# Hybrid encoder layer: four changes at the seams between stages, and three PSUM banks for scores with two for wide products

## Chip, cores and metric

One core of one Trainium2 chip runs the whole kernel. The metric is the device time of one execution in microseconds; of several executions the median is taken.

## What is computed

One layer of a bidirectional hybrid encoder on 1024 tokens of width 1024, all in float32:

```
h    = RMSNorm_pre(x);  z = h @ W_in   (q | f_fwd | f_bwd | i | g | u | v | gate_a | gate_b)
A    = bidirectional gated linear recurrence, 8 heads, 128x128 state per head (scores inside chunks, state between them)
Bm   = u * (128-position mixing matrix per channel group applied to LayerNorm(gelu(v)))
mix  = (sigmoid(gate_a) * (A @ W_a) + sigmoid(gate_b) * (Bm @ W_b)) @ W_out
x    = x + RMSNorm_post(mix)
x    = x + RMSNorm_post(SwiGLU(RMSNorm_pre(x)))            hidden width 2816
x    = x + (p @ W_ple) * sigmoid(x @ W_ple_gate)
```

## The kernel before

Every wide product keeps float32 accuracy with three matmuls: each operand is split into a high and a low part (`split_into`, L113 to L115: ScalarE copies the high part, VectorE subtracts for the low one), and `mm3` (L127) adds high-high, high-low and low-high. One 128x512 output with 1024 contracted elements is 24 matmuls.

PSUM has eight banks. `PS_BUFS` (L51) gives three to the tag mm, two to sc, one each to tr, st and o. `ps_any` (L58) hands wide products the tags mm, sc, mm, st, mm, sc in rotation; `wide_at` counts its uses, so whoever uses it shifts the tags of everything after.

The tile framework takes priorities from the order of the program, orders each engine's instructions with a simulation of its own, and gives buffers out as they come free in it. The order of an engine in the trace is therefore not that of the source, and on the chip each engine keeps to the order it was given. A pool on the left or right side of SBUF lies on the pools opened before it on that side; a tile of a new pool waits for the tiles that lay in the same place.

The stages, in order:

- **Opening.** `load_pw` (L318) loads and splits halves of p (transposed) and w_ple, 512 KB each, and `ple_product` (L392) makes 16 tiles of p @ W_ple from them, through the banks mm, st, mm, o. They are copied into four slots of `h32[1][1]` and stored to `pr_d`. `norm_x` (L345) normalises and transposes x through the sc banks.
- **Token-major products.** `tm_group` (L383) makes v (gelu, LayerNorm into vn), i, u and the second half of i. `u` and `vn` (L418) take the places of the split p and w_ple, u first. L439 to L445 mix positions and multiply into u.
- **First seam.** After the last `tm_group` (L447), L451 to L458 transpose u's eight tiles and split them into `bT`; `branch_b` (L468) loads a block of W_b, splits it and multiplies it with both halves of bT. The operands T1 to T4 of the next stage (L485 to L496) are made on VectorE in between. The memory of `raw` and `whl` (L460, L461) is where u and vn lay.
- **Columns and FFN gates.** `Seven.product` (L247) makes four 128x512 tiles from seven products of half the contraction (Strassen-Winograd), 12 matmuls each. X accumulates products 1, 6, 7, 4 in an mm bank, Y 5 and 3 in an sc bank, Z product 2 in `zbank` (st, tr, o in turn, L233). Product 1 and 2 need only original operands, product 5 needs T1, product 6 T2, product 7 T3 and product 4 T4. `begin` (L237) does products 1 and 2 ahead for the first two column pairs of the FFN.
- **Heads.** For each of 8 heads `scores` (L589) runs seven levels; a level is four matmuls of 128x128 per half (L612) into an sc bank, then VectorE updates QA (L621) and X (L624) in place or into a new buffer, merges the bank into SC (L634, for the two last levels ScalarE at L631), ScalarE copies the middle (L645) and GpSimd makes Y (L648). `proj` (L549) makes the next head's gates in four tiles through mm banks; ScalarE empties them at L579 and L580 into F, of which there is one buffer, and sk, of which there are two. `outputs` (L658) follows. In the last head `gate_a` (L726) fills in.
- **Merge.** `merge` (L762) multiplies with W_a (`whl` and `raw` have two buffers each) and loads W_out (`load_wo`, L777), whose split parts lie where the heads' buffers were. `mix_half` (L784), with `to_fm1` (L814) for the second half, normalises, adds x and transposes through the banks tr and o.
- **FFN and end.** L862 to L878 begin the first two column pairs and make T2, T3 and T4; then gates, down products, and the last gate.

Of the kernel before, what the change touches and what calls it, by code (L numbers as in the profile page):

```python
# [9 lines left out]
F32 = mybir.dt.float32  # L10
F32R = mybir.dt.float32r
# [6 lines left out]
P = 128  # L18
# [17 lines left out]
def kernel(ctx: ExitStack, tc: tile.TileContext, a: dict, out: bass.AP):  # L36
# [11 lines left out]
    dram = ctx.enter_context(tc.tile_pool(name="dram", bufs=1, space=DRAM))  # L48
    psum = ctx.enter_context(tc.tile_pool(name="psum", bufs=1, space=PSUM))

    PS_BUFS = {"mm": 3, "sc": 2, "tr": 1, "st": 1, "o": 1}  # L51
    wide = ["mm", "sc", "mm", "st", "mm", "sc"]
    wide_at = [0]

# [3 lines left out]
    def ps_any():  # L58
        tag = wide[wide_at[0] % len(wide)]
        wide_at[0] += 1  # L60
        return ps_tile(tag)

    def phase(name, bufs=1, side=None):
        pool = tc.tile_pool(name=name, bufs=bufs, reuse_waits="tile", **({"side": side} if side else {}))
        return pool, pool.__enter__()

    def close(*pools):
        for pool in pools:
            pool.__exit__(None, None, None)
# [3 lines left out]
    def t2(pool, role, bufs=2):  # L73
        return pool.tile([P, NH], F32, name=role, tag=role, bufs=bufs)
# [38 lines left out]
    def split_into(hi, lo, src, eng=None):  # L113
        nc.scalar.activation(hi, src, AF.Copy)  # L114
        (eng or nc.vector).tensor_tensor(out=lo, in0=src, in1=hi.bitcast(F32), op=ALU.subtract)  # L115
# [58 lines left out]
    class Seven:  # L174
# [59 lines left out]
            self.n += 1  # L234
            return ps_tile(self.zbanks[self.n % len(self.zbanks)])

        def begin(self, lhs, HB):  # L237

            X = ps_tile("mm")
            self.add(lhs, HB, 1, X, True)  # L240
            c11 = self.keep("p1", X)
            Z = self.zbank()
            self.add(lhs, HB, 2, Z, True)
            nc.vector.tensor_tensor(out=c11, in0=Z, in1=c11, op=ALU.add)
            return X, c11
# [41 lines left out]
    def pair(pool, name, tag):  # L287
# [4 lines left out]
    c_h32, p_h32 = phase("h32", side="right")  # L292
    h32 = [[p_h32.tile([P, 4, NH], F32, name=f"h32_{n}{g}") if n == 0 or g == 1 else None for g in range(2)]
           for n in range(2)]
    c_sgu, sgu = phase("sgu")
    masks = p01.tile([P, len(LEVELS), P], U8, name="masks")
    c_x, p0x = phase("p0x", 3)
    c_r, p0r = phase("p0r", 3)
    c_w, p0w = phase("p0w", 6)
    c_t, p0t = phase("p0t", 2)  # L300
# [17 lines left out]
    def load_pw(i, n):  # L318
        raw = praw[i][:, n]
        nc.sync.dma_start(raw, a[("pT", "w_ple")[i]][n])  # L320
        split_into(pwt[i][:, n, 0], pwt[i][:, n, 1], raw)

    load_pw(0, 0)
    load_x(0)
    load_pw(1, 0)
    nc.sync.dma_start(ident, a["ident"])
    gmix = p0x.tile([P, D], F32, name="gmix", bufs=1)
    nc.sync.dma_start(gmix, a["norm_mix_pre"].partition_broadcast(P))
# [40 lines left out]
    def ev_i(half):  # L369
        def f(t, ps):  # L370
            s = t2(p0t, "vs", 2)
            nc.scalar.activation(s, ps, AF.Copy)
            nc.sync.dma_start(v_d[half * 4:half * 4 + 4, :, t, :].rearrange("h p v -> p h v"),
                              s.rearrange("p (h v) -> p h v", h=4))
        return f
# [4 lines left out]
    def load_tm(gi, kk):  # L380
        return load_split(a["w_tm"][gi, kk], [2, NH], nc.gpsimd if kk % 2 else nc.vector, p0w, p0r)

    def tm_group(w, per_tile, ahead=None):  # L383

        for t in range(NT):
            ps = ps_tile(("mm", "st", "mm", "o", "mm")[t % 5]) if ahead is x_ahead else ps_any()
            mm3(ps, fm_lhs(hT[t // 4], t % 4), lambda p, k: w[k // 2][:, p, k % 2, :], KD)
            if ahead is not None:
                ahead(t)
            per_tile(t, ps)  # L390
# [24 lines left out]
    for t in range(4, NT):  # L415
        for e in range(2):
            ple_product(e, t)
    u, vn = [sgu.tile([P, NT, SGW], F32, name=name, tag="uv", bufs=2) for name in ("u", "vn")]  # L418

    def x_ahead(t):  # L420
        if t + 3 < NT:
# [11 lines left out]
    mf = p0x.tile([P, len(LEVELS), P], F32, name="mf", tag="xt")  # L433
    nc.sync.dma_start(mf, a["masks"])
    nc.vector.tensor_copy(masks, mf)
    tm_group(w, ev_i(0), layer_norm)
    w = [load_tm(2, kk) for kk in range(4)]
    tm_group(w, ev_u)
    for g in range(SGG):  # L439
        ps = ps_any()  # L440
        es = slice(g * SGE, (g + 1) * SGE)
        pv = ps.rearrange("p (c e) -> p c e", e=SGE)
        nc.tensor.matmul(pv, lhsT=wst[:, g, :], rhs=vn[:, :, es], start=True, stop=True)
        nc.vector.scalar_tensor_tensor(out=u[:, :, es], in0=pv, scalar=sgb[:, g:g + 1], in1=u[:, :, es],
                                       op0=ALU.add, op1=ALU.mult)  # L445
    w = [load_tm(3, kk) for kk in range(4)]
    tm_group(w, ev_i(1))  # L447
    close(c_t, c_w, c_r, c_x)


    c_b, p1b = phase("p1b", side="right")  # L451
    bT = [p1b.tile([P, 4, T], F32R, name=f"bT{p}") for p in range(2)]
    for t in range(NT):
        tp = ps_any()
        for i in range(4):
            nc.tensor.transpose(tp[:, i * P:(i + 1) * P], u[:, t, i * P:(i + 1) * P], ident)
        split_into(bT[0][:, :, t * P:(t + 1) * P], bT[1][:, :, t * P:(t + 1) * P],
                   tp.rearrange("p (k t) -> p k t", k=4))  # L458
    close(c_sgu)
    c_raw, rawp = phase("raw", 2)  # L460
    c_whl, whlp = phase("whl", 2)  # L461
# [3 lines left out]
    st1 = Seven(None, rawp, p1t, None, ("st", "tr", "o"))  # L465
    st1.first = whlp

    def branch_b(j):  # L468
        raw = rawp.tile([P, KD, P], F32, name="raw", tag="raw")
        nc.sync.dma_start(raw[:, 0:4], a["w_b"][j])  # L470
        wb = whlp.tile([P, 2, KD, P], F32R, name="whl", tag="whl")[:, :, 0:4]
        split_into(wb[:, 0], wb[:, 1], raw[:, 0:4])
        for n in range(2):
            ps = ps_any()
            mm3(ps, lambda p, k: wb[:, p, k, :], lambda p, k: bT[p][:, k, n * NH:(n + 1) * NH], 4)
            s = t2(p1t, "o", 2)
            nc.scalar.activation(s, ps, AF.Copy)
            nc.sync.dma_start(bw_d[j, :, n * NH:(n + 1) * NH], s)

    branch_b(0)  # L480
    branch_b(1)

    b11, b21, b22 = h32[0][0], h32[0][1], h32[1][1]
    b12 = [hT[1][p][0].bitcast(F32) for p in range(2)]
# [10 lines left out]
        nc.vector.tensor_tensor(out=sb[:, 1], in0=b21[:, k], in1=sa[:, 1], op=ALU.subtract)  # L495
        split_into(T4[0][:, k], T4[1][:, k], sb[:, 1])  # L496
    for j in range(2, KD):
        branch_b(j)
    close(c_b, c_h32)


    c_r, p1r = phase("p1r", 2)
# [234 lines left out]
    for h in range(H):  # L737
        nxt = Head()
        scores(h, cur)
        if h + 1 < H:  # L740
            proj(nxt, h + 1, "qfbg")
        if h == H - 1:

            gate_a(0)
            A0 = new_fm("A0")
            load_A(0, A0, range(H - 1), 5)
            gate_a(1)
            A1 = new_fm("A1")
        outputs(h, cur)
        cur = nxt  # L750
    load_A(1, A1, range(H - 1), 5)
# [9 lines left out]

    def merge(A):  # L762
        for j in range(KD):
            w = load_split(a["w_a"][j], [KD, P], None, whlp, rawp)
            for n in range(2):
                ns = slice(n * NH, (n + 1) * NH)
                ps = ps_any()
                mm3(ps, lambda p, k: w[:, p, k, :], fm_rhs(A[n]), KD)
                sg = t2(t3, "sg", 2)
                nc.sync.dma_start(sg, sig_d[j, :, ns])  # L770
                m0 = t2(t3, "y", 4)
                nc.sync.dma_start(m0, m0_d[j, :, ns])
                nc.vector.tensor_tensor(out=sg, in0=ps, in1=sg, op=ALU.mult)
                nc.vector.tensor_tensor(out=M[:, j, ns], in0=sg, in1=m0, op=ALU.add)
            load_wo(j)
# [84 lines left out]
    st4.w, st4.second, st4.t, st4.ev = s4w, s4r, t4, evp  # L860

    lhs = ahead[0]()  # L862
    begun = [st4.begin(lhs, HB2)]
    lhs1 = ahead[1]()
    begun.append(st4.begin(lhs1, HB2))

    b12, b22 = h1f
    for k in range(4):
# [199 lines left out]
```

## Time and profile before

| | |
|---|---|
| Median of 3 runs | 1988.57 us (1987.51 to 1992.4) |
| The profiled execution | 1992.11 us, of which the span of its instructions is 1990.3 us |
| TensorE, matmuls | 1926.7 us busy, 97% |
| TensorE, weight loads | 1604.8 us, 81%, beside the matmuls |
| VectorE, ScalarE, GpSimd | 56%, 38%, 10% |
| Mean granted TensorE clock | 0.989 |
| DMA | 201.87 MB, mean 101 GB/s |

The profile divides the span into 40 slices. TensorE is in its top tenth in nearly all of them; the slices that are lower are the first one, the stretch of the heads, and the seams. The granted clock is given in tenths of full speed, 2.4 GHz; 0.5 is 1.2 GHz.

### The profile page before, as it was taken

The numbers are of one execution on the slowest core, as the hardware profiler recorded it, in microseconds if no ns is written. First come the engines' busy times: TensorE is split into PE (matmuls) and PEld (weight loads), VectorE is DVE, ScalarE is ACT, GpSimd is POOL, SyncE is SP. The second block draws the span as 40 slices with busy tenths as digits, with TensorE's granted clock in tenths as the row PEclk, the third lists the DMA queues.
The fourth block names the chain that finished last, engine by engine and source line by source line (L and its number), as shares of the span: only waits on it lengthen the run. The fifth ranks groups of instructions, "written<-read, shape, count | busy, mean of one in ns | idle before, by whom it ended". The sixth has DMA issues, their size and how long they took to land.

```text
span 1990.3 us, 24039 instructions
## 1 busy us (share of the span) xinstructions
PE 1926.7 (97%) x9264; PEld 1604.8 (81%) x9264; DVE 1106.0 (56%) x1694; ACT 764.9 (38%) x1434; POOL 208.5 (10%) x153
## 2 busy tenths in 40 slices
PE   7999899999998999999999998999999999999999
PEld 6887788888887888888877886888888888888887
DVE  6401357545247777788754457855555536545743
ACT  7211244344344555445542146533333324213321
POOL 2600000000012222222112101000000000001000
PEclk9999899999999999999998998999999999999999
DMA  9120155433130112211336223232222205324232
GB/s 339 57 70 11 59 175 179 138 110 118 70 138 32 59 59 69 69 59 59 107 110 229 98 94 117 84 100 92 75 85 77 83 32 197 106 74 158 87 105 80
DMA packets 82147, 201.87 MB, mean 101 GB/s; under 512 B 8688, under 2 KB 17520, under 8 KB 82032
## 3 DMA queue, kind: packets, MB, share of 16 engines
q1 hardware_dynamic: 82032, 200.33, 30.0%
q8 instruction: 73, 1.20, 0.3%
q14 instruction: 42, 0.34, 0.1%
HBM read 147.35 MB, written 52.95 MB: 101 GB/s over the span
## 4 chain that ended last, share of the span: by engine, by line
PE 55%; DVE 5%; ACT 3%; issue 1%; DMA 1%; POOL 0%; DVEq 0%; SPq 0%; ACTq 0%; POOLq 0%
PE ps_mm L133 17%; PE ps_mm L280 12%; PE ps_sc L133 8%; PE ps_sc L280 6%; PE ps_st L133 4%; PE ps_sc L612 2%; DVE QA L621 1%; PE ps_tr L280 1%; PE ps_o L280 1%; PE ps_st L280 1%; DVE X L624 1%; PE ps_o L700 1%; DVE SC L634 1%; DVE F L654 1%; ACT SC L631 1%
## 5 line engine op out<-in xcount | busy, mean ns | idle before, releaser
L280 PE MATMUL ps_mm<-T,w 128*128 128x512 f32 x1296 | 310.1, 389 | 0.0
L280 PEld LDWEIGHTS ps_mm<-T,w 128*128 128x128 f32 x1296 | 243.2, 188 | 50.7 <-ACT u L230 0.2
L648 POOL TENSOR_TENSOR Y<-X,F 128x512 f32<-128x512 f32 x56 | 92.7, 1656 | 675.6 <-DVE F L587 401.8
L115 DVE TENSOR_TENSOR whl<-raw,whl 128x1024 fp32r<-128x1024 f32 (+1 forms) x70 | 85.5, 1225 | 132.0 <-ACT whl L114 132.0
L612 PE MATMUL ps_sc<-QA,X 128*128 128x128 f32 x896 | 125.5, 290 | 19.7 <-DVE QA L621 17.1
L115 DVE TENSOR_TENSOR w<-sums,w 128x1024 fp32r<-128x1024 f32 x72 | 88.1, 1223 | 92.8 <-ACT w L114 92.7
L612 PEld LDWEIGHTS ps_sc<-QA,X 128*128 128x128 f32 x896 | 115.1, 194 | 27.7 <-DVE QA L621 10.5
L133 PE MATMUL ps_mm<-whl,act 128*128 128x512 f32 x528 | 134.1, 389 | 0.0
L114 ACT ACTIVATE whl<-raw 128x1024 fp32r<-128x1024 f32 (+1 forms) x78 | 79.0, 1014 | 115.3 <-PE ps_sc L133 54.0
L133 PE MATMUL ps_mm<-hTa,whl 128*128 128x512 f32 x480 | 119.2, 396 | 0.0
L133 PE MATMUL ps_mm<-hTb,whl 128*128 128x512 f32 x480 | 117.8, 398 | 0.5 <-ACT F L580 0.5
L133 PEld LDWEIGHTS ps_mm<-whl,act 128*128 128x128 f32 x528 | 99.1, 188 | 20.7
L114 ACT ACTIVATE w<-sums 128x1024 fp32r<-128x1024 f32 x72 | 76.0, 1056 | 98.2 <-PE ps_sc L280 80.6
L280 PE MATMUL ps_sc<-T,w 128*128 128x512 f32 x432 | 108.5, 389 | 0.0
L621 DVE TENSOR_TENSOR QA<-QA,F 128x512 f32<-128x512 f32 x112 | 85.8, 767 | 34.1 <-PE ps_sc L612 33.5
L133 PEld LDWEIGHTS ps_mm<-hTb,whl 128*128 128x128 f32 x480 | 89.0, 189 | 18.7 <-ACT F L580 1.3
L133 PEld LDWEIGHTS ps_mm<-hTa,whl 128*128 128x128 f32 x480 | 88.4, 188 | 17.6 <-ACT F L580 0.2
L280 PEld LDWEIGHTS ps_sc<-T,w 128*128 128x128 f32 x432 | 81.1, 188 | 16.8
L133 PE MATMUL ps_sc<-whl,act 128*128 128x512 f32 x351 | 89.8, 390 | 0.0
L133 PEld LDWEIGHTS ps_sc<-whl,act 128*128 128x128 f32 x351 | 65.7, 188 | 13.8 <-ACT acc L927 0.2
L624 DVE TENSOR_TENSOR X<-X,F 128x256 f32<-128x256 f32 x112 | 74.6, 699 | 0.1
L645 ACT ACTIVATE X<-Y 128x512 f32<-128x512 f32 x56 | 36.1, 645 | 99.0 <-PE ps_sc L612 95.4
(311 smaller groups left out, 3566.7 us busy)
## 6 DMA issues: line engine op xcount, KB each, us to landing
raw<-in_w_fm_dram SPq DMA_DIRECT2D x52, 512.0 KB, 3.5
raw<-in_w_gate_dram SPq DMA_DIRECT2D x22, 512.0 KB, 3.4
raw<-in_w_up_dram SPq DMA_DIRECT2D x22, 512.0 KB, 3.9
act_d<-s SPq DMA_DIRECT2D x22, 512.0 KB, 2.9
raw<-in_w_down_dram SPq DMA_DIRECT2D x22, 512.0 KB, 3.8
raw<-act_d SPq DMA_DIRECT2D x22, 512.0 KB, 4.2
raw<-in_w_tm_dram SPq DMA_DIRECT2D x16, 512.0 KB, 5.6
pr_d<-h SPq DMA_DIRECT2D x16, 256.0 KB, 5.9
```

The costliest lines, as they stand in the source:

```text
L114: nc.scalar.activation(hi, src, AF.Copy)
L115: (eng or nc.vector).tensor_tensor(out=lo, in0=src, in1=hi.bitcast(F32), op=ALU.subtract)
L133: nc.tensor.matmul(ps, lhsT=lhs(lp, k), rhs=rhs(rp, k), start=(i == 0), stop=(i == n - 1))
L280: nc.tensor.matmul(ps, lhsT=lhs(lp, k), rhs=rhs(rp, k), start=(first and i == 0), stop=(i == n - 1), skip_group_check=True)
L612: nc.tensor.matmul(sp[:, i * P:(i + 1) * P], lhsT=X[:, c * P:(c + 1) * P], rhs=view(QA, c * P, [[2 * m, cb], [T + m, 2], [1, m]]), start=T ...
L621: nc.vector.tensor_tensor(out=view(QA, o, qd), in0=view(QA, o, qd), in1=view(F, of + 1, [[nb - 1, 2], [2, nb // 4], [0, m]]), op=ALU.mult)
L624: nc.vector.tensor_tensor(out=view(X2, o, dims), in0=view(X, o, dims), in1=view(F, nb + of + 1, [[4, nb // 8], [1 - nb, 2], [0, m]]), op=A ...
L631: nc.scalar.activation(SC[p0:p0 + m, 4 * g:4 * g + 4, c0:c0 + m], sp.rearrange("p (c t) -> p c t", c=4)[p0:p0 + m, :, c0:c0 + m], AF.Copy)
L634: nc.vector.copy_predicated(SC[:, 4 * g:4 * g + 4], masks[:, li, None, :].broadcast_to([P, 4, P]), sp.rearrange("p (c t) -> p c t", c=4))
L645: nc.scalar.activation(view(X2, m, mid), view(Y, m, mid), AF.Copy)
L648: nc.gpsimd.tensor_tensor(out=view(Y, m, mid), in0=view(X, m, mid), in1=view(F, 0, [[4, nb // 4], [nb + 3, 2], [0, m]]), op=ALU.mult)
L654: nc.vector.tensor_tensor(out=F2, in0=Fv[:, :, :, 0], in1=Fv[:, :, :, 1], op=ALU.mult)
```

## The change

Five edits:

1. The opening loads p and w_ple in four smaller transfers, in the order in which the first products need them, all ahead of the first tile of x.
2. u and vn change places; p0x moves to the right side and is closed after the masks; bT is made in two halves, the first ahead of the last `tm_group`, through tr and o instead of `ps_any`; `branch_b` is split into the load and the product, and the first two blocks do the first half of the tokens before the second.
3. The first two blocks of W_a are loaded before the last head's `outputs`.
4. `begin` takes its Z from st, then sc, instead of tr, then o.
5. mm has two banks and sc three.

```diff
-    PS_BUFS = {"mm": 3, "sc": 2, "tr": 1, "st": 1, "o": 1}
+    PS_BUFS = {"mm": 2, "sc": 3, "tr": 1, "st": 1, "o": 1}
...
-            Z = self.zbank()
+            Z = ps_tile(bank)
...
+    c_x, p0x = phase("p0x", 3, side="right")
     c_sgu, sgu = phase("sgu")
...
-    c_x, p0x = phase("p0x", 3)
...
-    load_pw(0, 0)
+    def piece(i, cut):
+        src, w, raw = a[("pT", "w_ple")[i]][0][:, cut[0], cut[1]], pwt[i][:, 0], praw[i][:, 0, cut[0], cut[1]]
+        nc.sync.dma_start(raw, src)
+        split_into(w[:, 0, cut[0], cut[1]], w[:, 1, cut[0], cut[1]], raw)
+    both, all_ = slice(0, 2), slice(0, NH)
+    piece(0, (both, slice(0, P)))
+    piece(1, (slice(0, 1), all_))
+    piece(1, (slice(1, 2), all_))
+    piece(0, (both, slice(P, NH)))
     load_x(0)
-    load_pw(1, 0)
...
-    u, vn = [sgu.tile([P, NT, SGW], F32, name=name, tag="uv", bufs=2) for name in ("u", "vn")]
+    vn, u = [sgu.tile([P, NT, SGW], F32, name=name, tag="uv", bufs=2) for name in ("vn", "u")]
...
+    close(c_x)
     tm_group(w, ev_i(0), layer_norm)
...
+    c_b, p1b = phase("p1b0", side="right")
+    bT = [pair(p1b, "bTa", None)]
+    def to_bT(n):
+        for t in range(4 * n, 4 * n + 4):
+            tp = ps_tile(("tr", "o")[t % 2])
+            for i in range(4):
+                nc.tensor.transpose(tp[:, i * P:(i + 1) * P], u[:, t, i * P:(i + 1) * P], ident)
+            ts = slice(t % 4 * P, (t % 4 + 1) * P)
+            split_into(bT[n][0][:, :, ts], bT[n][1][:, :, ts], tp.rearrange("p (k t) -> p k t", k=4))
+    to_bT(0)
     w = [load_tm(3, kk) for kk in range(4)]
     tm_group(w, ev_i(1))
-    close(c_t, c_w, c_r, c_x)
+    close(c_t, c_w, c_r)
...
+    c_b1, p1b1 = phase("p1b1", side="right")
+    bT.append(pair(p1b1, "bTb", None))
+    to_bT(1)
...
-    branch_b(0)
-    branch_b(1)
+    wb = [weight_b(j) for j in range(2)]
+    for n in range(2):
+        for j in range(2):
+            branch_b(j, wb[j], n)
...
             A1 = new_fm("A1")
+            wa = [load_split(a["w_a"][j], [KD, P], None, whlp, rawp) for j in range(2)]
         outputs(h, cur)
...
-            w = load_split(a["w_a"][j], [KD, P], None, whlp, rawp)
+            w = wa[j] if j < 2 else load_split(a["w_a"][j], [KD, P], None, whlp, rawp)
...
-    begun = [st4.begin(lhs, HB2)]
+    begun = [st4.begin(lhs, HB2, "st")]
     lhs1 = ahead[1]()
-    begun.append(st4.begin(lhs1, HB2))
+    begun.append(st4.begin(lhs1, HB2, "sc"))
```

## Rows read from the trace of the kernel before

**Rows 1.** The page: the span, and the engines' busy time.

```profile
span 1990.3 us, 24039 instructions
PE 1926.7 (97%) x9264; PEld 1604.8 (81%) x9264; DVE 1106.0 (56%) x1694; ACT 764.9 (38%) x1434; POOL 208.5 (10%) x153
```

**Rows 2.** Busy time by stretch: length, PE, PEld, DVE, ACT, POOL, clock, DMA share, GB/s.

```profile
24.00:40.40 16.40, 13.97 (x75) 10.90 (x74) 11.27 (x18) 14.04 (x30) 5.90 (x4) 1.00 1.02 375
229.18:248.47 19.29, 13.78 (x61) 10.97 (x60) 17.98 (x30) 10.93 (x20) 0.00 (x0) 0.73 0.26 82
...
743.80:796.85 53.05, 50.02 (x320) 44.10 (x320) 40.87 (x72) 27.78 (x71) 14.37 (x10) 1.00 0.19 65
1031.80:1066.00 34.20, 25.83 (x89) 19.35 (x89) 14.97 (x23) 14.11 (x37) 9.28 (x5) 0.80 0.61 201
1217.00:1242.00 25.00, 17.34 (x71) 13.62 (x70) 21.77 (x37) 15.76 (x35) 3.13 (x2) 0.80 0.43 145
1242.00:1262.00 20.00, 20.00 (x90) 16.58 (x89) 20.00 (x32) 11.03 (x17) 0.00 (x0) 1.00 0.01 1
```

**Rows 3.** Timeline, opening: start, us, instruction, [idle before <- releaser].

```profile
0.74 0.39 SPq L320 DMA_DIRECT2D praw<-in_pT_dram  x1
...
4.63 1.06 ACT L114 ACTIVATE pT<-praw 128x1024 fp32r<-128x1024 f32 x1 [2.61 <-DMA praw<-in_pT_dram]
...
5.59 0.61 ACT L108 ACTIVATE junk<-xt 128x512 f32<-128x512 f32 x1
...
7.46 1.06 ACT L114 ACTIVATE wp<-praw 128x1024 fp32r<-128x1024 f32 x1 [0.41 <-DMA praw<-in_w_ple_dram]
...
8.57 0.79 PE L133 MATMUL ps_mm<-wp,pT 128*128 128x512 f32 x1 [8.57 <-ACT wp L114]
```

**Rows 4.** Timeline, first seam.

```profile
232.75 0.69 DVE L115 TENSOR_TENSOR bT<-ps_mm,bT 128x512 fp32r<-128x512 f32 x1 [0.22 <-ACT bT L114]
...
233.50 0.66 PE L456 MATMUL ps_mm<-ident,u 128*128 128x128 f32 x4 [1.54 <-DVE bT L115]
...
235.80 6.39 SPq L470 DMA_DIRECT2D raw<-in_w_b_dram  x4
...
239.20 1.22 PE L133 MATMUL ps_mm<-bT,whl 128*128 128x512 f32 x2 [3.43 <-ACT whl L114]
```

**Rows 5.** Waits of PE in the heads, 560 to 1035 us: total, times, longest.

```profile
PE ps_sc L612 <- DVE QA L621: 17.1, 17, 1.6
...
PE ps_sc L612 <- ACT SC L631: 2.6, 6, 0.5
```

**Rows 6.** Timeline, one head of the steady pattern.

```profile
740.90 2.43 PE L133 MATMUL ps_mm<-hTa,whl 128*128 128x512 f32 x10
744.50 1.95 PE L601 MATMUL ps_sc<-q,ks 128*128 128x128 f32 x16
746.20 2.56 PE L133 MATMUL ps_mm<-hTa,whl 128*128 128x512 f32 x10
...
754.65 1.09 ACT L580 ACTIVATE F<-ps_mm 128x512 f32<-128x512 f32 x2 [0.19 <-DVE QA L621]
...
776.21 2.02 PE L612 MATMUL ps_sc<-QA,X 128*128 128x128 f32 x16 [1.26 <-DVE QA L621]
```

**Rows 7.** Timeline, merge.

```profile
1047.24 4.90 POOL L115 TENSOR_TENSOR wo<-raw,wo 128x1024 fp32r<-128x1024 f32 x2 [11.79 <-ACT wo L114]
...
1049.82 0.33 SPq L120 DMA_DIRECT2D raw<-in_w_a_dram  x1
...
1055.55 1.22 PE L133 MATMUL ps_mm<-A,whl 128*128 128x512 f32 x2 [3.96 <-ACT whl L114]
```

**Rows 8.** Timeline, start of the FFN.

```profile
1232.21 1.09 PE L820 MATMUL ps_tr<-ident,y 128*128 128x128 f32 x4 [6.94 <-DVE y L808]
...
1241.27 0.68 DVE L115 TENSOR_TENSOR T<-sg,T 128x512 fp32r<-128x512 f32 x1
...
1242.32 0.61 PE L280 MATMUL ps_mm<-B,wA 128*128 128x512 f32 x2
```

More of the change, by code (lines that the diff above doesn't have):

```diff
@@ L235, in zbank, with begin @@
             return ps_tile(self.zbanks[self.n % len(self.zbanks)])
-        def begin(self, lhs, HB):
+        def begin(self, lhs, HB, bank):
             X = ps_tile("mm")
@@ L445 @@
                                        op0=ALU.add, op1=ALU.mult)
+    c_b, p1b = phase("p1b0", side="right")
[8 more added lines that the diff above has]
+    to_bT(0)
     w = [load_tm(3, kk) for kk in range(4)]
     tm_group(w, ev_i(1))
-    close(c_t, c_w, c_r, c_x)
[L451 to L458, printed above, removed]
+    close(c_t, c_w, c_r)
+    c_b1, p1b1 = phase("p1b1", side="right")
+    bT.append(pair(p1b1, "bTb", None))
+    to_bT(1)
     close(c_sgu)
@@ L466, with weight_b @@
     st1.first = whlp
-    def branch_b(j):
+    def weight_b(j):
         raw = rawp.tile([P, KD, P], F32, name="raw", tag="raw")
@@ L472, in branch_b @@
         split_into(wb[:, 0], wb[:, 1], raw[:, 0:4])
[L473 to L478, printed above, removed]
-    branch_b(0)
-    branch_b(1)
+        return wb
+    def branch_b(j, wb, n):
+        ps = ps_any()
+        mm3(ps, lambda p, k: wb[:, p, k, :], lambda p, k: bT[n][p][:, k, :], 4)
+        s = t2(p1t, "o", 2)
+        nc.scalar.activation(s, ps, AF.Copy)
+        nc.sync.dma_start(bw_d[j, :, n * NH:(n + 1) * NH], s)
+    wb = [weight_b(j) for j in range(2)]
+    for n in range(2):
+        for j in range(2):
+            branch_b(j, wb[j], n)
     b11, b21, b22 = h32[0][0], h32[0][1], h32[1][1]
@@ L497 @@
     for j in range(2, KD):
-        branch_b(j)
-    close(c_b, c_h32)
+        wb = weight_b(j)
+        for n in range(2):
+            branch_b(j, wb, n)
+    close(c_b1, c_b, c_h32)
     c_r, p1r = phase("p1r", 2)
```

## The prediction

> **What bounds the kernel now.** I read the page first: TensorE's matmuls are busy for 1926.7 of 1990.3 us, and no other engine passes 81% [rows 1]. So the change can only pay where TensorE stands still or runs at a lower clock, 63.6 us of standing still over the whole span. Next I cut the span into stretches and looked for those where PE's busy time is shorter than the stretch or the clock is under 1 [rows 2]. The stretches left out there (columns, down products, FFN gates) are full. Five places remain; in each the timeline says which wait ends last.
>
> - Opening: no matmul before 8.57 us [rows 3], and 2.43 us of idle time between 24 and 40.4 us.
> - First seam, 229.18 to 248.47 us: 19.29 - 13.78 = 5.51 us idle, and the 13.78 us ran at a mean granted clock of 0.73 of 2.4 GHz, between its two levels, 1.2 and 2.4 GHz: some 13.78 x 0.27 = 3.7 us more. In all 9.2 us.
> - Heads: 53.05 us each in the steady pattern with 50.02 us of PE, 3.03 us idle. Of the named waits nearly all are for VectorE's QA, 17.1 us in 17 pieces, and only 2.6 us for a merge to empty a score bank [rows 5].
> - Merge, 1031.8 to 1066 us: 8.37 us idle, and 25.83 x 0.20 = 5.2 us for the clock.
> - Start of the FFN, 1217 to 1242 us: 7.66 us idle, and 17.34 x 0.20 = 3.5 us for the clock. From 1242 to 1262 us PE is full, and so is VectorE, 20.00 of 20 us [rows 2].
>
> That last row also prices a wide matmul at full clock: 90 in 20 us, 0.222 us each, 12 in 2.7 and 24 in 5.3.
>
> **Opening.** The first matmul waits for the second transfer's high part: p (512 KB, issued at 0.74) is being split at 4.63, x at 5.59, w_ple at 7.46, the matmul follows at 8.57 [rows 3]. Between the landings at 4.63 and 7.46 lie 1 MB, 0.36 MB per us. The first tile now needs 128 KB of p and 256 KB of w_ple instead of the 1.5 MB ahead of it: 1.1 MB less, 3.1 us, and a split of half the width, 0.61 instead of 1.06 us. So it starts at about 5.0, some 3.5 us earlier. Against this: x now stands behind 1 MB instead of 0.5 MB, 1.4 us later, with its norm and transposes; SP issues two more transfers at about 0.4 us each; and between 24 and 40.4 us ScalarE is busy 14.04 of 16.40 us and the DMA engines all of it [rows 2], so a PE that comes earlier finds banks not yet emptied, and has four of them for these products instead of five. I take 2 us of gain. Ends: +3.5 (all of it arrives) and -2 (nothing arrives, and the idle 2.4 us nearly double).
>
> The trace thus puts bytes ahead of everything. The Trainium skill's "DMA: Bandwidth & Descriptors", section Anatomy of one DMA, speaks against pieces: a fixed 2.0 us per transfer beside its bytes. If the two extra transfers paid that one after the other, 4 us, the opening would be 0.5 us slower instead of 2 us faster; no row here shows small loads queued like this.
>
> **First seam.** Three waits make the 5.51 us: transposes wait for VectorE's low parts 1.54 and 0.54 us, and the first product for its weights 3.43 us [rows 4]. The low parts came at 232.75 although ScalarE was long done: the memory of the low half lies where the last stored tile of i was, so the wait is for that store. The weights were issued at 235.80, since raw and whl lie on u. After the change half of the transposes hide under the last `tm_group`. Raw and the first whl buffer now lie on vn, which is dead by then, so block 0 is ready; the second whl buffer still lies on u. From the end of the last `tm_group` PE has two transposes and block 0's first half (2.7 us) at once, some 3.6 us. The second half of bT lies where that store is read from, so its high parts start 3.6 us after the end (232.75 - 229.18), four tiles through two banks take about 3 us more, u is free, and block 1's split (0.6 us each part) is ready about 6.6 us after the end. Idle: 6.6 - 3.6 = 3 us, less about 1 us for the two other transposes. So 2 us of 5.5 remain, and of the 3.7 us of clock about 2. Gain 5 us. Ends: +8 (almost all of it) and 0 (store and u pass the wait on whole). VectorE's operands for the next stage lie beside this and cost nothing as long as the eight blocks' products cover them, as now.
>
> **W_a ahead.** PE waits 3.96 us for block 2, not for block 0 or 1. Its load is issued at 1049.82, when GpSimd has finished the first of two splits of W_out that began at 1047.24 [rows 7]: both raw buffers held W_out, which waits for the heads' memory. With blocks 0 and 1 loaded earlier the two W_out loads still take both buffers ahead of block 2. Gain 0, ends -1 and +1; on SP the second load only changes places with a W_out load.
>
> **FFN start.** PE waits 6.94 us for y of the last tile [rows 8], and product 2 of the first two pairs stands behind it because Z needs tr and o, the transposes' banks. In st and sc these 24 matmuls, 5.3 us, run before: 1.6 us of this wait remain. But now they no longer cover what follows: T1's last low part starts at 1241.27, so after the transposes PE has some 8 us until product 5. Product 2 of the pairs 2 and 3 can come forward (5.3 us); about 2.7 us stay. Before, product 1 of pair 2 ran at 1242.32 in the third mm bank [rows 8]; now both mm banks are held by the two begun pairs, so 2.7 us of filler are gone while VectorE, full, finishes T2. VectorE in turn has two adds out of the way earlier. Against 7.66 + 3.5 us lost before I count 1.6 + 2.7 + 2.7 idle and some 2 for the clock: a gain of 2. Ends: +6 (VectorE's chain moves up by the adds and the early splits of the weights) and -3 (the idle time moves behind the transposes, the clock falls as before, and the filler is missing).
>
> **Banks.** In the column and FFN stages X of the next pair needs one other mm bank, and its predecessor's is emptied long before: 0. For the rotation of wide products the same bank comes back after four tiles of 2 to 5.3 us, against copies of 0.6 to 0.7 us: 0. In the heads it matters. With two score banks level 0 had to wait until the first scores were copied out; after the first scores at 744.50 PE took projection matmuls instead [rows 6]. A third lets level 0 follow at once, which shortens the chain of levels; but each level still needs VectorE's QA and X, and only a part of the waits is for banks. On the other side the projections lose a bank: two tiles stand full until F is free at 754.65, and the third bank is what the tile at 740.90 to 750 fills [rows 6]. With two banks that tile comes after 754.65, and the one that ran there moves to the end of the head, when the other pair is emptied: the same number of tiles between the same events, each one place later. I take 0.3 us of gain per head over 7 heads, 2 us. Ends: +21 (all 3.03 us x 7) and -22 (below).
>
> **Sum.** 2 + 5 + 0 + 2 + 2 = 11 us off 1992.1 us, the profiled execution: 1981. That execution is 3.5 us above the median of 1988.57, so the median after is 1977.5. A measurement of this kernel can tell about 0.3%, 6 us, from no change: faster is below 1982.6, slower above 1994.5.
>
> **Rivals.**
>
> 1. *Starved projections.* At the start of each head the ten and four matmuls that now run between the first scores and level 0, 14 x 0.222 = 3.1 us, find no bank and nothing takes their place; later they stand in the way of levels. Price 3.1 x 7 = 22 us. With the seams' 9 us and without my 2 the median is 2002. For it: the bank is really held, from about 741 to 755 us. Against: outputs and an earlier level 0 are there to run. It decides from 9 / 7 = 1.3 us per head, where the seams' gain is gone. Chance 0.14.
> 2. *The heads open up.* The repeated gaps come from bank shortage in the order itself, and all 3.03 us go: 21 us instead of 2, median 1959. For it: the same gaps in every head. Against: the row that names QA, 17.1 us. The Trainium skill's "Perfetto Trace Analysis", section Optimization Strategy, reads repeated equal gaps on the engine that should be full as a possible lack of buffers; by that rule this rival holds. The named releasers in the trace do not agree. Chance 0.10.
> 3. *The waits are passed on.* Store and u at the seam, ScalarE and DMA in the opening, VectorE at the FFN each hold the gain up to 1 or 2 us each, and the heads stay. The median is 1985 or so. For it: every one of these resources is full there. Chance 0.23.
>
> **How the numbers follow.** The forecast has 0.53, with its own range 1968 to 1986, of which about an eighth lies above 1982.6. Faster: 0.46 + 0.10 + a fifth of 0.23 = 0.61. Same: 0.07 + three quarters of 0.23 = 0.24, and 0.01 of rival 1. Slower: the rest, 0.14. The range leaves out most of rival 1 and half of rival 2: 1964 to 1993.
>
> **What would show it.** Opening: first matmul near 5 us, and the first 24-matmul tile of v starting near 38 instead of 40.4. Seam: weights of W_b issued before the last `tm_group` ends, one idle piece of about 2 us and not 3.43, the clock not long below 1. Merge: block 2 of W_a still waits some 4 us. FFN: a wait for y of 1 to 2 us, a new one for T1. Heads: period 52.5 to 53 us; level 0 directly after the first scores. The prediction is wrong if the period moves by more than 1 us, or if a full stretch (columns, FFN gates, down) shows idle PE because of two mm banks.

## The result: 53 us slower, and where they went

Median after: 2041.26 us of four runs (2040.15 to 2041.95), against 1988.04 us of four runs of the kernel before; ratio 1.0264, 95% interval 1.0251 to 1.0277. The forecast, 1977.5 us and a range of 1964 to 1993, had the wrong sign, and the range missed by 48 us.

The page after, to be read beside [rows 1]:

```profile
span 2039.7 us, 23973 instructions
PE 1945.7 (95%) x9264; PEld 1620.0 (79%) x9264; DVE 1118.3 (55%) x1696; ACT 764.8 (37%) x1436; POOL 202.3 (10%) x153
```

The 9264 matmuls are the same. The span grew by 49.4 us: 19.0 us in matmuls that ran slower, 30.4 us in which TensorE stood still. To see where, I cut both timelines at the same five pieces of work: the first column product, the first scores, the last head's scores, the first product of the FFN, the last matmul. Lengths in us, with the experiments that follow:

| | opening, token-major, first seam | columns | seven head periods | last head, merge | FFN to the last matmul |
|---|---|---|---|---|---|
| before | 286.7 | 297.4 | 372.6 | 261.4 | 767.5 |
| after | 295.6 | 297.8 | 386.1 | 282.5 | 772.9 |
| E1 seam changes alone | 292.1 | 297.4 | 370.3 | 260.4 | 765.5 |
| E2 banks alone | 293.9 | 297.8 | 386.0 | 282.6 | 772.4 |
| E3 mm 2, sc 2 | 295.2 | 297.8 | 393.8 | 269.2 | 774.1 |
| E4 mm 3, sc 3, o in st's bank | 295.0 | 297.4 | 383.3 | 271.4 | 778.6 |
| E5 third bank in the heads alone | 293.8 | 297.4 | 371.0 | 257.8 | 773.7 |
| E6 after, F 2, sk 4 | 294.5 | 297.8 | 390.3 | 257.5 | 773.9 |
| E7 before, F 2, sk 4 | 285.3 | 297.4 | 397.8 | 253.2 | 767.7 |
| E8 late edits alone | 286.5 | 297.4 | 372.4 | 259.5 | 765.7 |
| E9 real exchange | 290.9 | 297.4 | 370.3 | 259.6 | 765.2 |
| E10 mended | 286.3 | 297.4 | 370.2 | 260.1 | 764.8 |
| E11 fifth bank | 287.7 | 297.8 | 385.6 | 282.9 | 769.1 |
| E12 mended, tr in the opening | 283.4 | 297.4 | 370.4 | 259.7 | 765.5 |

After minus before: +8.9, +0.4, +13.6, +21.1, +5.4. The heads and the last head take 34.7 of the 49.4. The windows of these stretches (length, PE, PEld, DVE, ACT, POOL, granted clock, DMA share, GB/s; the second row ends where the closing merge begins), first before, then after:

```profile
584.15:956.73 372.58, 347.01 (x2169) 305.33 (x2168) 282.00 (x481) 191.08 (x472) 96.90 (x61) 0.99 0.18 61
956.73:1037.50 80.77, 76.26 (x477) 67.59 (x475) 51.64 (x95) 34.87 (x96) 12.58 (x11) 1.00 0.31 102
```

```profile
593.40:979.54 386.14, 343.53 (x2086) 304.26 (x2084) 283.38 (x476) 183.74 (x443) 88.86 (x59) 0.95 0.16 52
979.54:1083.07 103.53, 91.79 (x560) 80.62 (x559) 57.20 (x100) 43.16 (x125) 14.71 (x13) 0.97 0.32 105
```

Read the counts first. In the seven periods after, TensorE did 83 matmuls fewer in 13.6 us more; they came in the last head. Together both rows hold 2646 matmuls before and after. Idle time is 25.57 + 4.51 = 30.1 us before and 42.61 + 11.74 = 54.4 us after; busy time 423.3 and 435.3 us. So of 36.3 us 24.3 are waits, and 12.0 are longer busy time of the same matmuls, at a lower granted clock (0.95 and 0.97 instead of 0.99 and 1.00 of 2.4 GHz; a mean below 1 mixes the two levels).

The seven periods after take 55.9, 54.5, 57.3, 50.2, 53.4, 53.6 and 61.3 us, before 50.6, 56.4, 53.4 and then 53.0 to 53.1. The last and longest, 918.21 to 979.54, from TensorE's timeline (start, us, instruction, idle before and its releaser), to be read against [rows 6]:

```profile
910.86 5.28 PE L133 MATMUL ps_mm<-hTa,whl 128*128 128x512 f32 x22 [1.62 <-ACT F L602]
915.98 0.38 PE L722 MATMUL ps_o<-S,QA 128*128 128x128 f32 x2
...
918.21 1.95 PE L623 MATMUL ps_sc<-q,ks 128*128 128x128 f32 x16
919.92 0.71 PE L133 MATMUL ps_mm<-hTa,whl 128*128 128x512 f32 x2
920.46 5.39 PE L133 MATMUL ps_mm<-hTb,whl 128*128 128x512 f32 x23
...
928.60 0.39 PE L722 MATMUL ps_o<-S,QA 128*128 128x128 f32 x2
931.37 1.62 PE L634 MATMUL ps_sc<-QA,X 128*128 128x128 f32 x8 [2.38 <-DVE QA L616]
...
937.60 4.81 PE L133 MATMUL ps_mm<-hTa,whl 128*128 128x512 f32 x20
...
950.79 2.57 PE L133 MATMUL ps_mm<-hTb,whl 128*128 128x512 f32 x10
...
958.85 2.77 PE L634 MATMUL ps_sc<-QA,X 128*128 128x128 f32 x16 [2.16 <-DVE QA L643]
963.40 1.65 PE L698 MATMUL ps_st<-v,kt 128*128 128x128 f32 x6 [1.78 <-DVE S L704]
...
972.19 5.28 PE L133 MATMUL ps_mm<-hTa,whl 128*128 128x512 f32 x22 [1.62 <-ACT F L602]
```

and from ScalarE's timeline of the same period:

```profile
936.61 1.08 ACT L602 ACTIVATE F<-ps_mm 128x512 f32<-128x512 f32 x2
...
970.28 0.60 ACT L601 ACTIVATE sk<-ps_mm 128x512 f32<-128x512 f32 x1
...
972.51 0.61 ACT L602 ACTIVATE F<-ps_mm 128x512 f32<-128x512 f32 x1
```

Projection matmuls are the filler of the heads, and these rows show two holes in it. Two tiles are full by 926.2 and stay in both banks until F is free, 936.61; the next two are full at 953.4 and stay until 970.28 to 972.51. In between there is no projection to run. Before, a tile was being filled before and after the scores (740.90, 746.20) although L580 emptied two others only at 754.65 [rows 6]: that was the third bank.

But the kernel before has a long hole in every head too: after 770.93 no projection runs until 788.36. What differs is the other filler, the matmuls of `outputs`. Their last large group before, and the two long holes (columns as in the windows above), first before, then after:

```profile
780.74 0.39 PE L700 MATMUL ps_o<-S,QA 128*128 128x128 f32 x2
```

```profile
770.93:788.36 17.43, 15.19 (x122) 13.58 (x120) 13.82 (x24) 10.56 (x41) 5.92 (x5) 1.00 0.17 61
```

```profile
953.41:972.19 18.78, 13.21 (x91) 12.14 (x89) 16.93 (x32) 9.49 (x23) 3.53 (x3) 0.82 0.09 28
```

Of a head's 44 output matmuls, 42 ran from 770.77 to 781.13 before, in the long hole, and TensorE stood still for 2.24 us of it, at full clock. After, 42 of them run from 915.98 to 928.99, around the scores and beside the projections; the long hole holds none, TensorE stands for 5.57 us, and its mean clock is 0.82. The hole of the sixth period is as empty; those of the third and fourth still hold 42. So the outputs filled the time around the scores, and were then missing where the chain of levels is alone.

The outputs also hold up the next head. Its QA is made by VectorE, first after, then before:

```profile
929.02 2.29 DVE L616 TENSOR_TENSOR QA<-q,F 128x2048 f32<-128x2048 f32 x1
```

```profile
741.60 2.29 DVE L594 TENSOR_TENSOR QA<-q,F 128x2048 f32<-128x2048 f32 x1
```

QA has two buffers, and output matmuls of an earlier head read a QA until 928.99. The new QA starts just then, 10.8 us behind the scores, and level 0 waits for it (931.37); before, it was written ahead of the scores. In the last three heads after, QA starts 0.76, 0.04 and 0.03 us after the last output matmul that reads a QA. That the buffer is the reason is a reading of the times; no run tests it.

The seams after, from the timeline: the opening, the first seam, the merge and the start of the FFN.

```profile
6.33 3.23 PE L133 MATMUL ps_mm<-wp,pT 128*128 128x512 f32 x6 [6.33 <-ACT wp L114]
...
23.74 2.04 PE L133 MATMUL ps_mm<-wp,pT 128*128 128x512 f32 x6 [2.06 <-DVE h L408]
...
37.49 2.18 PE L133 MATMUL ps_mm<-wp,pT 128*128 128x512 f32 x6 [2.05 <-DVE h L408]
...
40.46 2.93 PE L133 MATMUL ps_mm<-wp,pT 128*128 128x512 f32 x6 [0.78 <-DVE h L408]
...
238.19 0.60 PE L462 MATMUL ps_tr<-ident,u 128*128 128x128 f32 x4
...
241.43 0.60 ACT L114 ACTIVATE bTb<-ps_tr 128x512 fp32r<-128x512 f32 x1 [2.40 <-DMA v_d<-vs]
...
242.81 0.78 PE L462 MATMUL ps_tr<-ident,u 128*128 128x128 f32 x4 [3.58 <-DVE bTb L115]
...
245.15 5.89 SPq L486 DMA_DIRECT2D raw<-in_w_b_dram  x4
...
248.43 1.22 PE L133 MATMUL ps_mm<-bTa,whl 128*128 128x512 f32 x2 [3.31 <-ACT whl L114]
...
1100.93 1.22 PE L133 MATMUL ps_mm<-A,whl 128*128 128x512 f32 x2 [3.68 <-ACT whl L114]
...
1276.79 0.63 PE L843 MATMUL ps_tr<-ident,y 128*128 128x128 f32 x4 [2.82 <-DVE y L831]
...
1280.23 4.88 PE L280 MATMUL ps_tr<-B,wA 128*128 128x512 f32 x12 [2.12 <-ACT h1f L845]
...
1288.06 1.22 PE L280 MATMUL ps_o<-B,wA 128*128 128x512 f32 x2 [2.48 <-ACT wA L114]
```

The first matmul is 2.2 us earlier than in [rows 3], but three waits for a bank to be copied out follow, 4.9 us. W_b's loads are issued after the transposes of u as in [rows 4], and the waits are no shorter: 3.58 us for the low parts (before 1.54 and 0.54) and 3.31 us for whl (before 3.43). Block 2 of W_a still waits, 3.68 us instead of 3.96 [rows 7]. The wait for y fell from 6.94 [rows 8] to 2.82 us, and two waits that were short or absent before take 4.6.

### The profile page after: what moved, and what is told of

Same layout as the page of the kernel before. It is cut to its first block, busy times and chain, and to the rows that moved or that the text cites. A ratio compares the mean times of both kernels' runs of the same rounds, so it can differ in the third digit from the quotient of the medians.

```text
span 2039.7 us, 23973 instructions
## 1 busy us (share of the span) xinstructions
PE 1945.7 (95%) x9264; PEld 1620.0 (79%) x9264; DVE 1118.3 (55%) x1696; ACT 764.8 (37%) x1436; POOL 202.3 (10%) x153
## 4 chain that ended last, share of the span: by engine, by line
PE 55%; DVE 5%; DMA 4%; ACT 3%; issue 1%; POOL 0%; DVEq 0%; SPq 0%; ACTq 0%
PE ps_mm L133 18%; PE ps_mm L280 12%; PE ps_sc L133 7%; PE ps_sc L280 6%; PE ps_st L133 3%; PE ps_sc L634 3%; PE ps_o L722 1%; DVE QA L643 1%; PE ps_o L280 1%; DMA raw<-in_w_ple_gate_dram 1%; PE ps_st L698 1%; PE ps_tr L280 1%; PE ps_st L280 1%; DMA raw<-act_d 1%; DVE X L646 1%
## 5 line engine op out<-in xcount | busy, mean ns | idle before, releaser
L280 PEld LDWEIGHTS ps_mm<-T,w 128*128 128x128 f32 x1296 | 243.3, 188 | 50.6 <-ACT u L230 0.2
L634 PE MATMUL ps_sc<-QA,X 128*128 128x128 f32 x896 | 134.1, 303 | 29.9 <-DVE QA L643 25.9
L634 PEld LDWEIGHTS ps_sc<-QA,X 128*128 128x128 f32 x896 | 122.9, 207 | 38.5 <-DVE QA L643 16.5
L646 DVE TENSOR_TENSOR X<-X,F 128x256 f32<-128x256 f32 x112 | 78.9, 740 | 0.5
```

What stands on the lines that cost most here:

```text
L280: nc.tensor.matmul(ps, lhsT=lhs(lp, k), rhs=rhs(rp, k), start=(first and i == 0), stop=(i == n - 1), skip_group_check=True)
L634: nc.tensor.matmul(sp[:, i * P:(i + 1) * P], lhsT=X[:, c * P:(c + 1) * P], rhs=view(QA, c * P, [[2 * m, cb], [T + m, 2], [1, m]]), start=T ...
L646: nc.vector.tensor_tensor(out=view(X2, o, dims), in0=view(X, o, dims), in1=view(F, nb + of + 1, [[4, nb // 8], [1 - nb, 2], [0, m]]), op=A ...
```

## Experiments

Theory: the loss is the third mm bank, in the opening, in the heads and at the FFN. Rivals: the seam changes alter the order of the heads; or the third sc bank does, by letting levels run ahead. E3, E4, E5, E6, E9 and E11 ran once each; the kernel before stood between 1986.5 and 1992.4 us in all its runs beside them.

**E1, E2: which half of the change.** E1 is the changed kernel with the banks of before, E2 the kernel before with the banks of after.

```diff
-    PS_BUFS = {"mm": 2, "sc": 3, ...}
+    PS_BUFS = {"mm": 3, "sc": 2, ...}      (E1; E2 the other way round)
```

> All four seam changes, with three banks for mm and two for sc as before. Theory (the missing mm bank costs nearly everything): 1980 to 1990 us; the opening's first 24-matmul tile of v starts before 42 us (after the change: 48.6), heads again 53 us each, last head back to its length of before. Rival (the seam changes themselves, through the order that they give): 2030 us or more, with the heads irregular.

> The kernel before with two banks for mm and three for sc and nothing else. Theory (the missing mm bank): 2030 to 2050 us, with irregular heads and a last head some 20 us longer. Rival (the seam changes): 1985 to 1995 us.

E1: 1993.68 us (ratio 1.0032, 1.0019 to 1.0045). E2: 2038.47 us (1.0252, 1.0232 to 1.0272). The seam changes are not what costs: with them the heads return to 53.0 to 53.3 us each from the third period on. E1 still misses its expectation of 1980 to 1990, because the seams' sum, forecast as 9 us of gain, is about zero: from the table the first column is 5.3 us longer, the last three 2.3, 1.0 and 2.1 us shorter. (The table has the profiled executions, 1992.19 us of E1 and 1992.11 us of the kernel before, which is above its median. By the medians E1 is 5.9 us slower than the kernel before, so the seam changes together cost some microseconds.) The tile of v that should start before 42 us started at 43.72.

**E3, E4: the missing mm bank or the added sc bank.** E3 has two of each and leaves a bank unused; E4 has three of each and puts the tag o into the bank of st.

```diff
-    PS_BUFS = {"mm": 2, "sc": 3, "tr": 1, "st": 1, "o": 1}
+    PS_BUFS = {"mm": 2, "sc": 2, "tr": 1, "st": 1, "o": 1}      (E3)
+    PS_BUFS = {"mm": 3, "sc": 3, "tr": 1, "st": 1}              (E4, ps_tile("o") gives st)
```

> The changed kernel with two banks for sc again, so that one bank of eight stands unused. Theory (what is missed is the third mm bank, and the third sc bank brings little): 2035 to 2060 us. Rival (the third sc bank does the harm, because levels run ahead of projections): 1985 to 2000 us.

> The changed kernel with three banks for mm and three for sc; the tag o uses the bank of st. Theory: the mm banks are back, so the opening and the heads' projections are as with the seams alone; the third sc bank is worth at most 2 us per head, and the shared bank costs up to that: 1975 to 2000 us. Rival (the third sc bank does the harm): 2020 us or more.

E3: 2036.67 us. So the third sc bank does not do the harm, and with two mm banks it is worth nothing: without it heads, last head and merge took 663.0 us, with it 668.6. E4: 2033.11 us, which misses the theory's 1975 to 2000 and falls to the rival. But its first three periods, 49.7, 54.4 and 53.0 us, stand beside 50.6, 54.3 and 53.3 in E1, the fourth takes 51.8, and only the last three grow to 56 to 59; and the products of outputs now share one bank. E4 changes two things at once and decides nothing about a third sc bank beside three mm banks.

**E5: the third bank given back to the heads alone.** mm 2, sc 2 and one bank x, used by `proj` and `gate_a` only.

```diff
-                ps = ps_tile("mm")
+                ps = ps_third()       # mm, mm, x in turn
```

> The changed kernel with two mm banks everywhere but for the projections of the heads and the gates of the last head, which take mm, mm and a third bank in turn; two banks for sc. Theory (the heads' projections starve with two banks): the seven head periods sum to 370 to 377 us (after the change 386, before 372.6), first to last stage of the merge as before, while the opening stays at 46 to 49 us and the start of the FFN stays 3 to 7 us longer; 1998 to 2010 us in all. Rival (what matters in the heads is the order that the other stages hand over, or the third bank elsewhere): 2025 us or more.

2000.28 us, 41 us less than after the change. The heads' rows (from the first scores to the last, and from there to the first product with A):

```profile
591.18:962.15 370.97, 345.63 (x2170) 304.43 (x2168) 282.00 (x481) 191.15 (x472) 96.57 (x61) 1.00 0.18 61
962.15:1010.70 48.55, 48.55 (x288) 43.08 (x287) 37.40 (x64) 19.83 (x46) 8.67 (x8) 1.00 0.30 104
```

2170 matmuls in 371 us at full clock, the order of the kernel before, with 42 output matmuls again in the long holes of the steady heads. Heads, last head and merge take 628.7 us instead of 668.6, and instead of 663.0 in E3, from which E5 differs by bank x alone. The FFN stretch stays 8.2 us longer than in E1, so the third bank is missed there too; the opening is between.

**E6, E7: banks that can be emptied sooner.** Two buffers for F and four for sk, in the changed kernel and in the kernel before.

```diff
-                s.F = hg.tile([P, 2, T], F32, name="F")
+                s.F = hg.tile([P, 2, T], F32, name="F", bufs=2)
...
-                sg = t2(t1, "sk")
+                sg = t2(t1, "sk", 4)
```

> The changed kernel, banks as changed, with two buffers for F and four for sk, so that ScalarE can empty the projections' banks before level 0 of the head is done. Theory (with two banks the projections stand still because both banks stay full until F is free): most of the 36 us that the heads and the last head lost come back, 2003 to 2018 us. Rival (the third bank matters as room for one tile more, whenever it is emptied): 2030 us or more.

> The kernel before, three mm banks, with two buffers for F and four for sk. If full banks already cost something with three of them (3.03 us idle per head), the heads shorten by up to 2 us each: 1972 to 1985 us. If they cost nothing then: 1985 to 1990 us.

E6: 2020.88 us, 3 us above what the theory expected. E7: 2006.25 us (1.0082, 1.0065 to 1.0099), outside both expectations: more buffers made the kernel before slower. From the first scores to the FFN, two mm banks instead of three cost 668.6 - 630.7 = 37.9 us with one F and two sk (after against E1). With two and four the difference is 647.8 - 651.0 = -3.2 us (E6 against E7), about nothing, since E6 has the seam changes too, which take 3.3 us off these stretches in E1. That agrees with a third bank whose worth in the heads is a place where a finished tile can wait for F and sk. It does not show it: both runs are 17 to 20 us slower there than E1, so a new limit that both share could hide a bank's worth. And the banks were not emptied sooner throughout. E7, one period, its window and its timelines, and the window of its long hole:

```profile
867.54:924.11 56.57, 51.13 (x320) 46.11 (x319) 40.20 (x72) 27.79 (x72) 12.10 (x9) 0.94 0.18 61
```

```profile
892.68 3.22 PE L133 MATMUL ps_mm<-hTa,whl 128*128 128x512 f32 x13
...
906.59 3.78 PE L612 MATMUL ps_sc<-QA,X 128*128 128x128 f32 x16 [4.23 <-DVE QA L621]
...
918.58 5.47 PE L133 MATMUL ps_mm<-hTb,whl 128*128 128x512 f32 x23
```

```profile
917.07 0.59 ACT L579 ACTIVATE sk<-ps_mm 128x512 f32<-128x512 f32 x1
```

```profile
895.90:918.58 22.68, 17.24 (x126) 16.16 (x126) 20.88 (x33) 11.25 (x36) 5.76 (x5) 0.85 0.24 82
```

ScalarE empties one tile at 871.39 and then none until 917.07. By 895.9 the projections have filled all three banks, and the next one starts at 918.58: they ran further ahead, and then the banks were full again. Of the 44 output matmuls 20 run before 895.9; the hole, 22.68 us long, keeps 22, and TensorE stands in it for 5.44 us at a clock of 0.85. The kernel before has 17.43 us, 2.24 us and 1.00. The period takes 56.57 us against 53.05.

**E8: the two late edits alone**, on the kernel before: blocks 0 and 1 of W_a ahead of the last outputs, and Z of `begin` in st and sc.

```diff
+            wa = [load_split(a["w_a"][j], [KD, P], None, whlp, rawp) for j in range(2)]
...
-            Z = self.zbank()
+            Z = ps_tile(bank)
```

> The kernel before with the two late edits alone: the first two blocks of W_a ahead of the last outputs, and the Z of begin in st and sc. From the run with all four seam changes and the banks of before (merge 1.0 us and FFN 2.1 us shorter than before, opening 3.3 and first seam 3.1 us longer): 1984 to 1987 us. Rival (the order in the simulation shifts, and the gains there came from the early edits): 1988 us or more.

1987.17 us, ratio 0.9986 (0.9977 to 0.9995). Both stretches gain 1.9 us each.

**E9, E10: the first seam.** In the built program u has the address 68416 and vn 84800 before and after the change, and raw starts at 68416: the exchange in the source exchanged nothing, since each tile took the buffer that came free for it. E9 gives u and vn tags of their own, and takes the four pieces of the opening out; E10 also opens the pool of junk, c and vs ahead of the weights. Both have three mm and two sc banks.

```diff
-    vn, u = [sgu.tile([P, NT, SGW], F32, name=name, tag="uv", bufs=2) for name in ("vn", "u")]
+    vn, u = [sgu.tile([P, NT, SGW], F32, name=name, tag=tag) for name, tag in (("vn", "uv0"), ("u", "uv1"))]
...
-    c_r, p0r = phase("p0r", 3)                               (E10)
-    c_w, p0w = phase("p0w", 6)
-    c_t, p0t = phase("p0t", 2)
+    c_t, p0t = phase("p0t", 2)
+    c_w, p0w = phase("p0w", 6)
+    c_r, p0r = phase("p0r", 3)
```

> The run with all four seam changes and the banks of before, less the four pieces in the opening (loads as before), and with u and vn tied to their places, so that vn really lies under raw and the first whl buffer. If the pieces cost the 3.3 us of the opening, the first 24-matmul tile of v starts at 40.4 us again; if something else of the change does (p0x on the right side), at 43 to 44. If W_b was late because u never left its place, its loads are now issued before the last tile of i is stored, the wait of 3.3 us for whl is under 1 us, and from v's first tile to the first product of W_b pass 198 to 199.5 us (before 198.8, with the seam changes 201.9); if it was late for another reason, 201 to 202.

> The run above, with the pool of junk, c and vs opened ahead of the weights, so that the second half of bT lies on raw tiles of long ago and not on the last stored tile of i. If that store holds bT's high parts (2.4 us on ScalarE, 3.6 us on TensorE), TensorE stands for under 2 us in the first seam, 195 to 198 us from v's first tile to the first product of W_b, and the whole takes 1977 to 1984 us with the late edits' 3 us. If the wait has another cause, 1984 to 1988 us.

E9: 1989.90 us; v's first tile at 42.36, so 1.4 us of E1's 3.3 go with the pieces. (In E10, which moves the pools too, it starts at 41.11, so another 1.2 us go with their order.) From there to the first product of W_b pass 200.9 us, between the two expectations. The seam in E9:

```profile
234.16 11.91 SPq L478 DMA_DIRECT2D raw<-in_w_b_dram  x4
...
240.51 2.18 ACT L114 ACTIVATE T<-sums 128x512 fp32r<-128x512 f32 x4
242.59 1.14 ACT L114 ACTIVATE whl<-raw 128x512 fp32r<-128x512 f32 x2
...
243.26 1.22 PE L133 MATMUL ps_mm<-bTa,whl 128*128 128x512 f32 x2 [3.28 <-ACT whl L114]
```

W_b's loads are now issued 1.3 us after the first transposes, not 7 (245.15 against 238.19 after the change), so the place was what held them. The wait for whl is 3.28 us all the same, against the "under 1 us" expected: on ScalarE four splits of T, 2.18 us, stand ahead of it, and whl's split follows them without a gap. A freed wait was passed on to the engine's own order.

E10: 1986.01 us of 11 runs, ratio 0.9989 (0.9980 to 0.9998), above the 1977 to 1984 expected with a mended seam. The wait for the store is gone:

```profile
232.33 0.59 ACT L114 ACTIVATE bTb<-ps_tr 128x512 fp32r<-128x512 f32 x1
...
233.70 0.66 PE L454 MATMUL ps_tr<-ident,u 128*128 128x128 f32 x4 [1.08 <-DVE bTb L115]
...
238.84 1.22 PE L133 MATMUL ps_mm<-bTa,whl 128*128 128x512 f32 x2 [3.28 <-ACT whl L114]
```

bTb's high part now follows the transposes at once, and TensorE waits 1.08 instead of 3.79 us (E9) for it; with whl's 3.28 and a wait of 0.54 the seam keeps 4.9 us idle, not under 2. From v's first tile to W_b's first product pass 197.7 us (before 198.8, E1 201.9), inside the 195 to 198 expected.

**E11: a bank more where tr is free.** The changed kernel, mm 2, sc 3.

```diff
-        ps = ps_tile(("mm", "st", "mm", "o")[t % 4])
+        ps = ps_tile(("mm", "st", "tr", "o")[t % 4])      (tm_group with x_ahead likewise)
...
-    begun.append(st4.begin(lhs1, HB2, "sc"))
+    begun.append(st4.begin(lhs1, HB2, "sc", "sc"))       (X in sc too)
```

> The changed kernel, banks as changed, but the opening's products go through mm, st, tr and o (tr has no other use there), five banks in all as before, and the second begun pair of the FFN takes its X from the third sc bank. Theory (two mm banks cost in the opening and the FFN because a product more must wait for its bank): v starts at 43 to 45 us instead of 48.6, and the stretch from the FFN's first product to the end is 4 to 7 us shorter than after the change; the heads stay as after the change, so 2028 to 2033 us. Rival (those stretches are slower through the order or the DMA queues): both unchanged, 2038 to 2043 us.

2029.66 us. Up to the first column product 287.7 instead of 295.6 us, 7.9 of the 8.9 us lost there. That is a bank's worth, but not only that of the missing one: alone, the two mm banks cost 7.1 us there (E2) and the seam edits 5.3 (E1), and a bank more helps with three mm banks too (E12). (Its order changed as well, a tile of v ran at 34.5, ahead of the last products of the opening, so that landmark tells nothing here.) The FFN stretch came down by 3.8 us, a little less than the 4 to 7 expected. The heads stayed, as expected.

**E12: E10 with tr in the opening.** Three mm banks, two for sc.

```diff
-        ps = ps_tile(("mm", "st", "mm", "o")[t % 4])
+        ps = ps_tile(("mm", "st", "tr", "o")[t % 4])      (tm_group with x_ahead likewise)
```

> The mended run (three mm banks, loads of the opening as before, vn really under W_b's buffers, junk, c and vs ahead of the weights, the two late edits) with the opening's products and the first token-major tiles through mm, st, tr and o, so that tr serves too. If banks still limit the opening with three mm banks, the first column product starts 1 to 3 us earlier than in the mended run (286.3) and the whole takes 1982 to 1985 us; if the DMA engines set the opening's end (97% busy in the kernel before), nothing moves: 1985 to 1988 us.

1984.41 us of 11 runs (1982.56 to 1985.73), ratio 0.9980 (0.9971 to 0.9989): the fastest here, 3.7 us under the kernel before. The first column product starts at 283.4, 2.9 us earlier than in E10, which differs by tr alone (the order of the opening moved with it). So even with three mm banks the opening waited for banks, and the DMA engines were not its only bound.

## Why the prediction was wrong

- **Banks, the step that failed.** "The same number of tiles between the same events, each one place later", and from it 2 us of gain. The step looked at projections and score banks and took the rest of the order as it was. The number did not hold: the seven periods have 83 matmuls fewer, which come in the last head. Nor did the rest: in the rows above, the outputs run around the scores and the long hole is left with 5.57 us idle at a clock of 0.82 instead of 2.24 at 1.00. The measured loss is 34.7 us from the first scores to the FFN, and E1, E2, E3 and E5 show that it hangs on the third bank of the projections. Why the framework's order gave up the outputs' old place is not shown.
- **Rival 1** had the sign, and the hold from 741 to 755 us was in the rows. Its mechanism was not quite what happened: 26 projection matmuls still ran between the scores at 918.21 and level 0 (919.92 to 926.2). I gave it 0.14 because "outputs and an earlier level 0 are there to run". The outputs did run there, and were missing later; the level 0 was not early, it waited for QA at 931.37. Its price of 22 us was short of 34.7: it left out the lower clock, 12.0 us up to the closing merge, and the last head, whose gates use the same banks. The 0.3 us per head for a third sc bank are not borne out (E3).
- **Opening.** Forecast 2 us of gain, ends +3.5 and -2. The first matmul came 2.2 us earlier, not 3.5. With three mm banks v starts 3.3 us later, with two 8.2 us later, both beyond the lower end. I named the four banks and did not price them; the waits for h L408, 4.9 us, are part of that price, and in E11 the stretch is 7.9 us shorter. The Trainium skill's rule of a fixed 2.0 us per transfer ("DMA: Bandwidth & Descriptors", Anatomy of one DMA, which gives it for transfers issued by GpSimd; these are issued by SyncE) did not decide. The first split of the small piece of p starts at 3.35, after an issue at 0.74, and that of the fourth transfer at 7.63:

```profile
3.35 0.42 ACT L114 ACTIVATE pT<-praw 128x256 fp32r<-128x256 f32 x1 [1.34 <-DMA praw<-in_pT_dram]
...
7.63 0.84 ACT L114 ACTIVATE pT<-praw 128x768 fp32r<-128x768 f32 x1 [0.69 <-DMA praw<-in_pT_dram]
```

  128 KB took 2.6 us here and 512 KB 3.9 us in [rows 3], so by these two a fixed part of some 2.2 us is there (an estimate: 384 KB more took 1.3 us more), but the four overlap: the fourth was in use 4.3 us after the first.
- **First seam.** Forecast 5 us, the lower end 0; in E1 the way from v's first tile to the columns took 2.0 us more. The step "raw and the first whl buffer now lie on vn" was false, and with the place mended "so block 0 is ready" was too, for ScalarE's order. That the second half of bT would wait some 3.6 us for the store was about right (3.2 us, 241.43 against 238.19).
- **W_a ahead.** The mechanism was right: block 2 still waits, 3.68 us. From the last scores to the FFN, E1 gains 1.0 and E8 1.9 us, at and above the upper end of 1.
- **FFN start.** The size was right with three banks: 2 us forecast, 2.1 us in E1 and 1.9 in E8. The missing X bank was priced at 2.7 us inside that sum; the two mm banks cost this stretch 7.5 us (after against E1), of which a bank for X gives back 3.8 (E11).
- **Columns.** Right, 0.4 us.
- The Trainium skill's reading of repeated gaps as a possible lack of buffers ("Perfetto Trace Analysis", Optimization Strategy), rival 2, did not help in the heads: a third sc bank beside two mm banks brought nothing (E3), and more buffers for F and sk made the kernel before 17 us slower there (E7). In the opening one bank more did bring 2.9 us (E12).

Open: what a third sc bank is worth beside three mm banks; the last 0.7 us of the opening in E10; and how far the heads with two mm banks, and those of E6 and E7, are set by the framework's order of the outputs rather than by banks and buffers, since no run held that order fixed.

## What to carry to other kernels

Before taking a buffer from independent work that fills another chain's waits, list when each of its buffers becomes full and what empties it, and ask what the engine has left to run between these times. Do this for every kind of filler: when one kind loses its place, another is moved there and is missing where it was. Filler is worth most where the chain is alone; running it sooner can cost too (E7, 17 us from the first scores to the FFN). After a change that moves a tile, look up its address; a pool gives out what is free, not what the source's order suggests.

## What the runs showed of the hardware

The length of the gaps alone does not set the granted clock. The second head period (from the second scores to the third) stands still as long in the kernel before as in E1, 5.53 and 5.60 us, but the granted clock was 0.94 in one and 1.00 in the other. The windows, first before, then E1:

```profile
634.73:691.14 56.41, 50.88 (x311) 44.95 (x310) 40.94 (x68) 27.51 (x70) 14.44 (x10) 0.94 0.18 61
```

```profile
640.07:694.40 54.33, 48.73 (x312) 43.08 (x311) 40.95 (x68) 27.48 (x70) 14.44 (x10) 1.00 0.19 64
```

The matmuls took 50.88 and 48.73 us: 2.1 us of difference come with the clock alone. That is also all of E1's gain in the heads (372.6 to 370.3), so it says nothing for the seams.
